# A tuned decoder trunk on one core: kept sums for a second set of seven products, and a norm row made three units later

## The chip, the cores and the metric

The kernel runs on one core of one Trainium2 chip. The metric is the device time of one execution in microseconds, from the first to the last instruction of the core with what lies around it. TensorE (PE) multiplies matrices, VectorE (DVE) and ScalarE (ACT) work on tiles elementwise, GpSimd (POOL) and SyncE (SP) mostly issue transfers here.

## The reference

Two layers over 256 tokens of width 2048. Layer 0 mixes with chunked gated linear attention, layer 1 with forgetting attention, whose keys, values and forget gates come from a projection of the normed stream between the layers. Each layer ends with a gated MLP, 5632 wide, with a causal convolution of width 3 between the up projection and the gate. All is float32.

```python
def fox_shared_kv(x, g_kv, w_kv, b_f):
    hs = rmsnorm(x, g_kv)
    k, v, fl = split_cols(hs @ w_kv, [FOX_WIDTH, FOX_WIDTH, FOX_HEADS])
    ...

def conv_ffn(h, w_up, conv_w, conv_b, w_down):
    u = causal_dwconv(h @ w_up, conv_w, conv_b)
    a, val = split_cols(u, [FFN_HIDDEN, FFN_HIDDEN])
    return (jax.nn.silu(a) * val) @ w_down

def reference(x, ...):
    for i in range(DEPTH):
        if i == N_A_LAYERS:
            fk, fv, fc = fox_shared_kv(x, fox_kv_norm, fox_w_kv, fox_b_f)
        ...
        h = rmsnorm(x, norm_ffn[i])
        x = x + conv_ffn(h, ffn_w_up[i], ffn_conv_w[i], ffn_conv_b[i], ffn_w_down[i])
    return rmsnorm(x, norm_final)
```

## The kernel before

**Products in three.** Every float32 operand is held as a rounded high part and the rest, its low part, and a product is three matmuls: high by high, low by high, high by low. Activations are split once. Weights arrive from memory in units of 512 KB (128 x 1024) and are split as they come: ACT casts the raw unit to `whi` (L229, or L377 in a set of seven), DVE subtracts to get `wlo` (L230, L378). PE reads both as the moving operand, 512 columns a matmul.

**An up pair.** The up projection is made in 11 pairs a layer, j = 0, 4, ..., 40, each by `pair_steps`. A pair has 16 input chunks of 128, so 16 units, and fills four results of 128 tokens x 512 columns; a plain unit is 12 matmuls. They lie in accumulator banks named p1 to p7 and x. The banks take turns from pair to pair, so that in some pairs p1 is printed as `acc` and in others as `ps_o`.

**A set of seven products.** At chunk 6 (SEVEN_UP) two units go together: 2 x 2 blocks of tokens and columns over two input chunks are multiplied with seven block products instead of eight, 21 matmuls instead of 24. It needs sums of the inputs (`usum`, made once a layer by `input_sums` and `token_sums`) and of the weights: the units land in `ra` and `rb` (`raw2`, two buffers in turn), the first halves are cast as w1 (512 columns) and w2, then four DVE subtractions (L427 to L430) turn `ra` and `rb` into block differences, which are cast as w3 and w4. So a set has four casts at L377 instead of two at L229. Its products p1, p5, p6, p7 have banks of their own. After a pair's last set `early` runs: two ACT copies of bank p1 (L1472 plain, L1473 scaled), four DVE adds that combine p6, p7 and p5 (L1474 to L1477), three ACT scales (L1479). At the pair's end `late` adds the results (L1483), and DVE transposes them (L1435).

**A second set.** The first pair after each part's down pairs (j = 20 and j = 32) has one more set, at chunk 11 (`more`, SEVEN_MORE). For it the sums of chunks 11 and 12 are made anew each time, in the buffer of a down projection's sums (`dsum0`): twice a layer.

**Work beside.** What follows the up projection (24 convolution taps on ACT at L1384, adds at L1391, silu L1397, product L1404, the splits L516 and L517, sums L672 and L673) is handed out in small steps by `tick(share)` while PE works on the next pairs. `drive` gives a share of 1.45 a unit.

**What sets the order.** The program is put in order by a scheduler that simulates the engines before anything runs. Work inside `tc.high_priority(offset=AHEAD)` is placed earlier, `tc.issue_after` sets a floor. Each engine then executes its list in that order. The order of ACT's list around a set is therefore an outcome of that simulation, and a small edit can reorder it.

**The norm row.** The projection for the shared keys (`two_tm([fk(0), fk(1)], ...)`, then `fk(2)`) needs the norm of the stream only when its results are read. `nx.row` (L589 to L598) spreads the norm over partitions: DVE builds a diagonal `dg` twice, PE multiplies it with ones into `ps_t`, ACT copies `row` out. Before it is hooked behind unit 2 of `fk(1)`.

## Time and profile before

| | before |
|---|---|
| three runs, us | 2221.61, 2224.04, 2224.32 (median 2224.04) |
| the profiled execution, us | 2221.88, its span 2220.1 |
| PE busy, us | 2207.2 (99%) in 10323 instructions |
| DVE busy, us | 1788.5 (81%) |
| ACT busy, us | 1418.8 (64%) |
| POOL busy, us | 136.1 (6%) |
| granted TensorE clock, mean | 0.999 |

The span runs from the first to the last instruction, so it is 1.8 us shorter than the execution's own time. In a row of the profile `L402 PE MATMUL acc<-whi,B` reads: line 402, engine, operation, the tile written and the tiles read, without buffer numbers. `whi` and `wlo` are weights, `B`, `A`, `mix` and `more` split activations, `usum` and `dsum` sums of them. A busy time is a sum over instructions; matmuls overlap, so a group's mean of 389 ns is not the time from one start to the next.

### The profile page before, as it was taken

What the parts mean: (1) busy time and instruction counts of PE and PEld (TensorE: products, weight loads), DVE (VectorE), ACT (ScalarE), POOL (GpSimd) and SP (SyncE); (2) the same over time, 40 slices, a digit from 0 to 9 for tenths busy, and PEclk for the clock granted to TensorE, in tenths of its full rate; (3) what the DMA queues carried; (4) which work ended last, traced back from release to release, by engine and by line L of the source; (5) the groups of instructions that cost most, each with busy time, mean ns of one, the idle gap of its engine ahead of it and who ended that gap; (6) DMA issues with size and microseconds to landing.
All of it is one profiled execution on the core that took longest, in us unless ns stands there. A gap on an engine that the chain in (4) does not pass through costs nothing.

```text
span 2220.1 us, 30058 instructions
## 1 busy us (share of the span) xinstructions
PE 2207.2 (99%) x10323; PEld 1853.8 (84%) x10323; DVE 1788.5 (81%) x2654; ACT 1418.8 (64%) x2257; POOL 136.1 (6%) x257
## 2 busy tenths in 40 slices
PE   9999999999999999999999999999999999999998
PEld 7888888888888888888887998888888888888886
DVE  7768977688897888888978569668888888888896
ACT  6655664556787468656865455555787647665874
POOL 0000000001100000001110000000101000100100
PEclk9999999999999999999999999999999999999999
DMA  9767667778777567667777767777677757766674
GB/s 356 245 223 222 192 191 242 248 231 253 229 243 258 185 221 244 227 225 240 226 250 244 233 203 244 224 240 244 218 240 246 240 196 239 234 236 222 225 258 150
DMA packets 165633, 515.47 MB, mean 232 GB/s; under 512 B 20700, under 2 KB 41832, under 8 KB 165480
## 3 DMA queue, kind: packets, MB, share of 16 engines
q1 hardware_dynamic: 148488, 461.36, 63.6%
q0 software_dynamic: 16416, 51.40, 7.6%
q8 instruction: 81, 1.33, 0.2%
q10 hardware_dynamic: 576, 0.79, 0.1%
q14 instruction: 72, 0.59, 0.1%
HBM read 469.68 MB, written 43.79 MB: 231 GB/s over the span
## 4 chain that ended last, share of the span: by engine, by line
PE 95%; issue 2%; DVE 1%; DMA 1%; ACT 0%; POOL 0%; DVEq 0%; ACTq 0%; POOLq 0%
PE acc L402 30%; PE acc L333 23%; PE ps_s L402 15%; PE ps_o L402 7%; PE ps_t L402 7%; PE acc L305 3%; PE acc L260 3%; PE acc L363 2%; PE acc L258 1%; PE ps_s L333 1%; DVE wlo L230 0%; PE ps_s L1011 0%; DMA raw<-wp 0%; DMA fvt<-far 0%; PE ps_o L686 0%
## 5 line engine op out<-in xcount | busy, mean ns | idle before, releaser
L230 DVE TENSOR_TENSOR wlo<-raw,whi 128x1024 fp32r<-128x1024 f32 (+4 forms) x739 | 876.8, 1196 | 256.6 <-ACT whi L229 232.6
L229 ACT ACTIVATE whi<-raw 128x1024 fp32r<-128x1024 f32 (+4 forms) x739 | 760.4, 1037 | 447.4 <-PE acc L333 166.3
L333 PE MATMUL acc<-whi,B 128*128 128x512 f32 (+3 forms) x1248 | 292.0, 370 | 0.0
L377 ACT ACTIVATE whi<-raw 128x1024 fp32r<-128x1024 f32 (+1 forms) x136 | 129.8, 954 | 190.7 <-PE acc L402 75.5
L333 PEld LDWEIGHTS acc<-whi,B 128*128 128x128 f32 x1248 | 227.1, 188 | 28.0
L378 DVE TENSOR_TENSOR wlo<-raw,whi 128x1024 fp32r<-128x1024 f32 (+1 forms) x136 | 148.0, 1091 | 63.3 <-ACT whi L377 58.8
L402 PE MATMUL acc<-whi,mix 128*128 128x512 f32 x764 | 194.6, 389 | 0.0
L402 PE MATMUL acc<-whi,B 128*128 128x512 f32 x750 | 193.0, 389 | 0.0
L402 PEld LDWEIGHTS acc<-whi,mix 128*128 128x128 f32 x764 | 143.3, 188 | 30.2 <-ACT whi L229 0.2
L402 PEld LDWEIGHTS acc<-whi,B 128*128 128x128 f32 x750 | 140.8, 188 | 29.6
L333 PE MATMUL acc<-wlo,B 128*128 128x512 f32 (+3 forms) x624 | 158.6, 369 | 0.0
L333 PEld LDWEIGHTS acc<-wlo,B 128*128 128x128 f32 x624 | 114.6, 188 | 14.5
L1384 ACT ACTIVATE tap<-yzu,cw 128x256 f32<-128x256 f32 x264 | 123.5, 531 | 1.5 <-DMA yzu<-far 1.5
L1384 ACT ACTIVATE tap<-fvt,cw 128x256 f32<-128x256 f32 x264 | 123.3, 529 | 0.8 <-DMA fvt<-far 0.8
L1391 DVE TENSOR_TENSOR tap<-tap,tap 128x1024 f32<-128x1024 f32 x88 | 107.3, 1219 | 1.1 <-ACT tap L1384 1.0
L402 PE MATMUL acc<-wlo,mix 128*128 128x512 f32 x382 | 107.5, 389 | 0.0
L402 PE MATMUL acc<-wlo,B 128*128 128x512 f32 x375 | 107.3, 389 | 0.0
L402 PE MATMUL ps_s<-whi,mix 128*128 128x512 f32 x386 | 106.1, 389 | 0.0
L402 PE MATMUL ps_s<-whi,B 128*128 128x512 f32 x342 | 93.5, 389 | 0.0
L402 PEld LDWEIGHTS ps_s<-whi,mix 128*128 128x128 f32 x386 | 72.5, 188 | 15.3
L402 PEld LDWEIGHTS acc<-wlo,mix 128*128 128x128 f32 x382 | 71.7, 188 | 15.0
L402 PEld LDWEIGHTS acc<-wlo,B 128*128 128x128 f32 x375 | 70.4, 188 | 14.7
(498 smaller groups left out, 3802.3 us busy)
## 6 DMA issues: line engine op xcount, KB each, us to landing
raw<-wp SPq DMA_DIRECT2D x743, 512.0 KB, 4.5
fvt<-far POOLq DMA_DIRECT2D x100, 128.0 KB, 5.3
raw<-wp SPq DMA_DIRECT2D x32, 384.0 KB, 3.5
far<-yu POOLq DMA_DIRECT2D x22, 512.0 KB, 5.8
far<-yzu POOLq DMA_DIRECT2D x22, 512.0 KB, 5.4
yzu<-far POOLq DMA_DIRECT2D x88, 128.0 KB, 5.0
raw<-wp SPq DMA_DIRECT2D x24, 388.0 KB, 4.7
x<-xtok SPq DMA_DIRECT2D x8, 512.0 KB, 6.6
```

Of the source, the lines that this page charges most:

```text
L229: casts.append(S.activation(hi[:, s], raw[:, s], AF.Copy))
L230: lows.append(V.tensor_tensor(lo[:, s], raw[:, s], hi[:, s].bitcast(F32), ALU.subtract))
L258: mm = TE.matmul(acc[p][c][:, :T], w[:, s], both[:, 0, :], start=False, stop=end and j == 3)
L260: mm = TE.matmul(acc[p][c], w[:, s], both, start=u == j == 0, stop=end and j == 3)
L305: mm = TE.matmul(acc[b][:, :n], src[kcs[j] - base][:, part, b * P : (b + 1) * P], w, start=u == 0 and low == part == j == 0, stop=u == end ...
L333: mm = TE.matmul(acc[b][:, :n], src[kc - base][:, part, b * P : (b + 1) * P], ready[low][:, j * n : (j + 1) * n], start=i == low == part = ...
L363: mm = TE.matmul(acc[b][:, :n], src[kc - base][:, part, b * P : (b + 1) * P], w, start=i == low == part == j == 0, stop=i == end and low = ...
L377: casts.append(S.activation(hi[:, :n], src, AF.Copy))
L378: lows.append(V.tensor_tensor(lo[:, :n], src, hi[:, :n].bitcast(F32), ALU.subtract))
L402: r = TE.matmul(bank[name], x, w, start=name not in begun, stop=last)
L1384: S.activation(by_run(taps[i][:, s, c, i:]), zs[slot][:, :, 2 * c + s], AF.Copy if i else AF.Identity, bias=0.0 if i else w[3], scale=w[2 ...
L1391: V.tensor_tensor(taps[0], taps[0], taps[n][:, :, :, :T], ALU.add)
```

## The change

1. `MORE_IN = (1, 5, 6, 8, 9)`: the pairs j = 4, 20, 24, 32 and 36 have a set at chunk 11 beside the one at chunk 6. Before, only 20 and 32 had. So j = 4, 24 and 36 are new, in both layers.
2. The sums of chunks 11 and 12 are made once a layer, at unit 13 of pair 0, into a tile of their own (`usum11`) that stays for the layer. The two makings a layer into `dsum0` go.
3. Pairs in `MORE_IN` hand out the work beside with a share of 1.7 instead of 1.45.
4. For room, the mask's part that only the linear attention uses is a tile `gmask` of that stage's pool, loaded on POOL's queue instead of SP's.
5. `nx.row` runs after unit 3 of `fk(2)`, instead of after unit 2 of `fk(1)`.

```diff
--- before.py
+++ after.py
@@ -35,6 +35,7 @@
 SEVEN_UP = (6,)
 SEVEN_DOWN = {4: 0, 10: 1, 20: 0, 34: 1}
 SEVEN_MORE = 11
+MORE_IN = (1, 5, 6, 8, 9)
 
 
 LEVELS = (64, 16, 4)
@@ -157,11 +158,10 @@
 
     gains = const.tile([P, G_N], F32, name="gains")
     part = const.tile([P, C_N], F32, name="part")
-    mask = const.tile([P, M_N], F32, name="mask")
+    mask = const.tile([P, M_SCAN], F32, name="mask")
     ident = mask[:, M_ID : M_ID + P]
     ones = mask[:, M_ONE : M_ONE + P]
     foxmask = mask[:, M_FOX : M_FOX + T]
-    scanmask = mask[:, M_SCAN : M_SCAN + T]
 
     def gain(name, i):
         c = C_GAIN[name] + i
@@ -808,7 +808,7 @@
                     for i in range(KC):
                         nc.sync.dma_start(xf[i], xt[i])
                     nc.sync.dma_start(part, par)
-                    nc.sync.dma_start(mask[:, M_FOX:], msk[:, M_FOX:])
+                    nc.sync.dma_start(mask[:, M_FOX:], msk[:, M_FOX:M_SCAN])
         with tc.issue_after(nrm.made.ins):
             for i in range(KC):
                 split(bufB, i, xf[i], gain("mix0", i))
@@ -833,6 +833,8 @@
         h, mix = bufB, bufA
         with tc.tile_pool(name="gla", bufs=1) as gp:
             scratch[0] = gp
+            gmask = gp.tile([P, M_N - M_SCAN], F32, name="gmask")
+            nc.gpsimd.dma_start(gmask, msk[:, M_SCAN:])
 
             ks = [place("A", 8 + i, "ks", F32) for i in range(2)]
             gq1, gk1 = place("A", 10, "gq1", F32), place("A", 11, "gk1", F32)
@@ -882,7 +884,7 @@
                     mz = gp.tile([P, T], F32, name="gm", tag="tmp", bufs=5)
                     V.tensor_scalar(mz, ps[:, :T], bias, 0.0, ALU.add, ALU.min)
                     V.tensor_tensor(mz, mz, e, ALU.subtract)
-                    V.tensor_tensor_scan(bc[:, c, :], scanmask, mz, 0.0, ALU.mult, ALU.add)
+                    V.tensor_tensor_scan(bc[:, c, :], gmask[:, :T], mz, 0.0, ALU.mult, ALU.add)
                 return bc
 
 
@@ -1030,12 +1032,13 @@
                 for b in range(2):
                     S.activation(a3[:64, b, 64:], ps[64 * b : 64 * (b + 1), P : P + 64], AF.Copy)
                 ins = inside[hd % 2]
-                eye = mask[:, M_EYE:].bitcast(I32).unsqueeze(1).to_broadcast(ins.shape)
+                eye = gmask[:, M_EYE - M_SCAN :].bitcast(I32).unsqueeze(1).to_broadcast(ins.shape)
                 V.copy_predicated(ins, eye, ps[:, 192:320].rearrange("p (b t) -> p b t", b=2))
                 for li, B in enumerate(LEVELS):
                     H = B // 4
                     p3 = levels[li].rearrange("p (b c) -> p b c", b=2)
-                    m3 = mask[:, M_LVL + NVER * li : M_LVL + NVER * (li + 1)].bitcast(I32)
+                    at0 = M_LVL - M_SCAN + NVER * li
+                    m3 = gmask[:, at0 : at0 + NVER].bitcast(I32)
                     o4 = ins.rearrange("p b (n t) -> p b n t", t=B)
                     for i, (o, w) in enumerate(VERSIONS):
                         og = o4[:, :, :, (i + 1) * H :]
@@ -1162,11 +1165,12 @@
             def query_input(i):
                 split_turned(hq, i, (*stash, spare[1])[i // 4], "mix1")
 
-            two_tm([fk(0), fk(1)], 8, 2, {(1, 2): nx.row,
-                                          (1, 3): lambda: nx.land(spare[1]), (1, 5): nx.take})
+            two_tm([fk(0), fk(1)], 8, 2, {(1, 3): lambda: nx.land(spare[1]), (1, 5): nx.take})
             step = fk(2)
             for u in range(8):
                 step(u)
+                if u == 3:
+                    nx.row()
                 query_input((u + 12) % KC)
             cs = fp.tile([P, T], F32, name="fc")
             cc = fp.tile([P, 2, FOX_H], F32, name="fcc")
@@ -1411,12 +1415,12 @@
 
             product = [None]
 
-            def input_sums(k, tag="usum", at=None):
+            def input_sums(k):
 
                 r = fp.tile([P, 2, T], F32, name="cv", tag="cv")
                 for s in range(2):
                     V.tensor_tensor(r[:, s, :], h[k + s][:, 0, :].bitcast(F32), h[k + s][:, 1, :].bitcast(F32), ALU.add)
-                t = held(tag, k if at is None else at)
+                t = held("usum", k)
                 token_sums(r, t)
                 return t
 
@@ -1461,7 +1465,10 @@
                     credit[0] -= cost
                     step()
 
-            def up_pair(j, more={}):
+            def sets_of(j):
+                return (*SEVEN_UP, SEVEN_MORE) if j // 4 in MORE_IN else SEVEN_UP
+
+            def up_pair(j):
 
                 count[2] += 1
                 turns = [turn(j + 2 * h_, 8) for h_ in range(2)]
@@ -1483,26 +1490,29 @@
                         V.scalar_tensor_tensor(u[b, h_], a, scale(b), u[b, h_], ALU.mult, ALU.add)
                     turns[h_](b, u[b, h_])
 
-                return pair_steps(where["up", l, j], h, {**up_sums, **more}, count[2] % 2, pool, early, late)
+                return pair_steps(where["up", l, j], h, {k: up_sums[k] for k in sets_of(j)}, count[2] % 2, pool, early, late)
 
             def first(k):
                 {2: lambda: nx.land(landing[0]), 3: nx.take, 8: nx.col,
                  9: lambda: nx.land(landing[1]), 11: nx.take}.get(k, int)()
+                if k == 13:
+                    up_sums[SEVEN_MORE] = input_sums(SEVEN_MORE)
                 tick(0)
 
             def drive(steps, share=1.45):
                 for k in steps:
                     tick(share if k >= 0 else 0.0)
+
+            def drive_up(j):
+                drive(up_pair(j), 1.7 if j // 4 in MORE_IN else 1.45)
 
             up_sums = {k: input_sums(k) for k in SEVEN_UP}
             for k in up_pair(0):
                 first(k)
             done = 4
-            more = {}
             for p, (lo, hi) in enumerate(PARTS[:-1]):
                 while done < hi + 4:
-                    drive(up_pair(done, more))
-                    more = {}
+                    drive_up(done)
                     done += 4
                 src = [m[c % RING] for c in range(lo, hi)]
                 for f in (0, 2):
@@ -1510,11 +1520,9 @@
                     drive(down_pair(l, p, f, src, {c - lo: t for c, t in sums.items() if f}, count[2] % 2, pool,
                                     lambda: (temps(0), temps(1))))
                 sums.clear()
-                more = {SEVEN_MORE: input_sums(SEVEN_MORE, "dsum", 0)}
             lo, hi = PARTS[-1]
             while done < hi:
-                drive(up_pair(done, more))
-                more = {}
+                drive_up(done)
                 done += 4
             p = len(PARTS) - 1
             src = [m[c % RING] for c in range(lo, hi)]
```

The lines move by 7 from the FFN on: L1384 becomes L1388, L1397 becomes L1401, L1472 and L1473 become L1479 and L1480, L1479 becomes L1486. In the listings below a name's buffer number may differ between the kernels (`raw_5469` before is `raw_5488` now).

**ACT's list, the set at chunk 6 of the third up pair (j = 8) of layer 0.** The pair before it, j = 4, has one set before and two now. The rows at L377 are the casts of w1 (512 columns), w2, w3 and w4, in this order; L1472/L1473 (now L1479/L1480) are the copies of the pair's own bank p1. Before:

```order
L377 ACTIVATE whi<-raw_5469 128x512
L377 ACTIVATE whi<-raw_5470 128x1024
L1397 ACTIVATE tap_4575<-tap_4575 128x2x256
L516 ACTIVATE mix_3451<-cv 128x256
L516 ACTIVATE mix_3458<-cv 128x256
L377 ACTIVATE whi<-raw_5469 128x1024
L377 ACTIVATE whi<-raw_5470 128x1024
L229 ACTIVATE whi<-raw 128x1024
L1384 ACTIVATE tap_4576<-fvt,cw 128x4x2x32
L1384 ACTIVATE tap_4577<-fvt,cw 128x4x2x32
L1384 ACTIVATE tap_4576<-fvt,cw 128x4x2x32
L1472 ACTIVATE fvt<-ps_o 128x512
```

Now:

```order
L377 ACTIVATE whi<-raw_5488 128x512
L377 ACTIVATE whi<-raw_5489 128x1024
L1401 ACTIVATE tap_4577<-tap_4577 128x2x256
L1479 ACTIVATE fvt<-ps_o 128x512
L1480 ACTIVATE fvt<-ps_o,ny 128x512
L377 ACTIVATE whi<-raw_5488 128x1024
L516 ACTIVATE mix_3453<-cv 128x256
L516 ACTIVATE mix_3460<-cv 128x256
L377 ACTIVATE whi<-raw_5489 128x1024
L229 ACTIVATE whi<-raw 128x1024 x2
```

Both copies of p1, which stood behind w4 and a further cast, now stand ahead of w3; the splits at L516 stand between w3 and w4. The sets of j = 8 and j = 40 have this order in both layers.

**The same place of the other following pair, j = 28 of layer 0** (j = 28 of layer 1 reads the same). Now:

```order
L377 ACTIVATE whi<-raw_8040 128x512
L377 ACTIVATE whi<-raw_8041 128x1024
L1479 ACTIVATE fvt<-acc 128x512
L1480 ACTIVATE fvt<-acc,ny 128x512
L1401 ACTIVATE tap_4577<-tap_4577 128x2x256
L377 ACTIVATE whi<-raw_8040 128x1024
L672 ACTIVATE dsum<-cv 128x512
L377 ACTIVATE whi<-raw_8041 128x1024
```

Here the silu stands between the copies and w3, and a sum of the down projection (L672) between w3 and w4.

**The second set of a new two-set pair (j = 4 of layer 0).** Now:

```order
L377 ACTIVATE whi<-raw_5217 128x512
L377 ACTIVATE whi<-raw_5218 128x1024
L377 ACTIVATE whi<-raw_5217 128x1024
L1479 ACTIVATE fvt<-acc 128x512
L1480 ACTIVATE fvt<-acc,ny 128x512
L377 ACTIVATE whi<-raw_5218 128x1024
```

The copies stand behind w3 and ahead of w4 here. That is also the order in six sets of the kernel before, j = 12 and j = 28 of layer 0 among them.

**PE's list at the set of j = 8, layer 0.** `B_105` and `B_106` are chunks 6 and 7. The rows `ps_o<-whi,B_105` and `ps_o<-wlo,B_105` are product p1 (w1), `B_106` and the first `usum` rows into `acc` are w2, `ps_s<-whi,usum` is w3, `ps_t<-whi,usum` and the following `acc<-whi,B_106` are w4. Before:

```order
L402 MATMUL acc<-whi,B_104 128x512 x8
L402 MATMUL acc<-wlo,B_104 128x512 x4
L402 MATMUL ps_o<-whi,B_105 128x512 x2
L402 MATMUL ps_o<-wlo,B_105 128x512
L402 MATMUL acc<-whi,B_106 128x512 x2
L402 MATMUL acc<-wlo,B_106 128x512
L402 MATMUL acc<-whi,usum 128x512 x2
L402 MATMUL acc<-wlo,usum 128x512
L402 MATMUL ps_s<-whi,usum 128x512 x4
L402 MATMUL ps_t<-whi,usum 128x512 x2
L402 MATMUL acc<-whi,B_106 128x512 x2
L402 MATMUL ps_s<-wlo,usum 128x512 x2
```

Now:

```order
L402 MATMUL ps_o<-whi,B_105 128x512 x2
L402 MATMUL acc<-wlo,B_103 128x512 x4
L402 MATMUL acc<-whi,B_104 128x512 x8
L402 MATMUL acc<-wlo,B_104 128x512 x4
L402 MATMUL acc<-whi,B_106 128x512 x2
L402 MATMUL acc<-whi,usum 128x512 x2
L402 MATMUL ps_o<-wlo,B_105 128x512
L402 MATMUL acc<-wlo,B_106 128x512
L402 MATMUL acc<-wlo,usum 128x512
L402 MATMUL ps_s<-whi,usum 128x512 x4
L402 MATMUL ps_t<-whi,usum 128x512 x2
L402 MATMUL acc<-whi,B_106 128x512 x2
```

The last matmul of p1, `ps_o<-wlo,B_105`, has moved behind the first rows of w2: from it to the first matmul of w3 it is now 3 matmuls (7 before), and to the first of w4 7 (11 before).

**PE's list at the norm row.** Before, in `fk(1)`:

```order
L333 MATMUL acc<-whi,B_111 128x512 x2
L333 MATMUL acc<-whi,B_112 128x512 x2
L333 MATMUL acc<-whi,B_111 128x512 x2
L596 MATMUL ps_t<-dg,onesr 128x256
L333 MATMUL acc<-whi,B_112 128x512
L596 MATMUL ps_t<-dg,onesr 128x256
L333 MATMUL acc<-whi,B_112 128x512
```

Now, in `fk(2)`, some 90 matmuls later:

```order
L333 MATMUL acc<-wlo,B_106 128x512
L333 MATMUL acc<-wlo,B_105 128x512
L333 MATMUL acc<-wlo,B_106 128x512
L596 MATMUL ps_t<-dg,onesr 128x256 x2
L333 MATMUL acc<-whi,B_107 128x512 x2
L333 MATMUL acc<-whi,B_108 128x512 x2
```

The two L596 matmuls left the middle of a unit and stand between two units.

## The prediction

> **What bounds the kernel now.** I read the page's first part, then the chain of waits, then the windows of single up pairs, then the timeline around one set.
>
> ```profile
> span 2220.1 us, 30058 instructions
> PE 2207.2 (99%) x10323; PEld 1853.8 (84%) x10323; DVE 1788.5 (81%) x2654; ACT 1418.8 (64%) x2257; POOL 136.1 (6%) x257
> ...
> PE 95%; issue 2%; DVE 1%; DMA 1%; ACT 0%; POOL 0%; DVEq 0%; ACTq 0%; POOLq 0%
> ```
>
> PE is busy in 2207.2 of 2220.1 us, and 95% of the chain is PE. So a matmul that goes is a gain, and a wait that PE did not have is a loss, nearly one for one. There is little else: all idle time of PE together is 12.9 us.
>
> ```profile
> 758.30:800.80 42.50, 42.50 (x188) 34.96 (x188) 33.80 (x38) 22.95 (x26) 0.00 (x0) 1.00 0.57 191
> 800.80:843.80 43.00, 43.00 (x191) 35.51 (x190) 35.22 (x44) 32.66 (x52) 5.50 (x10) 1.00 0.79 248
> 843.80:886.80 43.00, 43.00 (x191) 35.53 (x190) 37.31 (x45) 32.79 (x53) 5.47 (x10) 1.00 0.74 236
> 935.10:977.50 42.40, 42.40 (x188) 34.99 (x187) 39.05 (x50) 20.74 (x24) 0.00 (x0) 1.00 0.69 228
> 1020.50:1063.40 42.90, 42.90 (x190) 35.43 (x189) 38.05 (x49) 32.87 (x53) 5.46 (x10) 1.00 0.77 246
> ```
>
> The columns are the window, its length, then busy time and count of PE, PEld, DVE, ACT and POOL, and the clock. These are up pairs of layer 0, from one pair's first matmul to the next pair's: j = 20 and j = 32 (42.5 and 42.4 us, two sets), j = 24, 28 and 40 (43.0, 43.0 and 42.9, one set). PE fills every one of them. What the reader must also see is ACT: 22.95 and 20.74 us in the two-set pairs, some 33 in the others. The same windows for the convolution taps alone (L1384 on ACT):
>
> ```profile
> 758.30:800.80 42.50, 0.00 (x0) 1.00 0.57 191
> 800.80:843.80 43.00, 11.21 (x24) 1.00 0.79 248
> 935.10:977.50 42.40, 0.00 (x0) 1.00 0.69 228
> ```
>
> The pairs with two sets carried no taps; the new ones do. So DVE and ACT have not yet been seen under both loads at once.
>
> **The gain of a second set.** It replaces 24 matmuls by 21, of which 12 read the sums.
>
> ```profile
> 857.78 1.07 PE L402 MATMUL ps_s<-whi,B 128*128 128x512 f32 x4
> 858.69 0.61 PE L402 MATMUL ps_t<-whi,B 128*128 128x512 f32 x2
> 862.11 1.10 PE L402 MATMUL acc<-whi,usum 128*128 128x512 f32 x4
> 863.05 0.63 PE L402 MATMUL acc<-wlo,usum 128*128 128x512 f32 x2
> ```
>
> Four plain matmuls take 858.69 - 857.78 = 0.91 us, 0.227 each; four on sums 863.05 - 862.11 = 0.94, 0.235 each. A set therefore gains 3 x 0.227 - 12 x 0.008 = 0.58 us, which is what the windows differ by (0.5 to 0.6). Six new sets: **-3.5 us**. Bounds: 0.5 and 0.6 each, -3.0 to -3.6.
>
> **The gain of the norm row.**
>
> ```profile
> PE ps_t L596 <- DVE dg L594: 2.0, 1, 2.0
> ```
> ```profile
> 1199.94 1.52 PE L333 MATMUL acc<-whi,B 128*128 128x512 f32 x6
> 1203.46 0.38 PE L596 MATMUL ps_t<-dg,onesr 128*128 128x256 f32 x1 [2.00 <-DVE dg L594]
> 1204.27 1.09 PE L333 MATMUL acc<-wlo,B 128*128 128x512 f32 x4
> ```
> ```profile
> 1200.36 1.23 DVE L230 TENSOR_TENSOR wlo<-raw,whi 128x1024 fp32r<-128x1024 f32 x1
> 1201.57 1.23 DVE L230 TENSOR_TENSOR wlo<-raw,whi 128x1024 fp32r<-128x1024 f32 x1
> ```
>
> Six matmuls from 1199.94 at 0.227 end their turn at 1201.30; the next starts at 1203.46. The gap is 2.16 us, and it waits for DVE's diagonal. Moved behind unit 3 of fk(2), some 90 matmuls or 20 us later, the row finds it ready: DVE's own order is unchanged there. What would be late next are the weights: the `wlo` read at 1204.27 was done at 1201.59, so 2.68 us ahead; 2.16 earlier it is still 0.5 ahead, and the next, done at 1202.80, is read eight matmuls later, at 1202.11 + 1.82 = 1203.9. I take the whole **-2.2 us**; if that slack is eaten, the bound is -1.1.
>
> **The cost: two waits in the pair after each new one.** This is the term that decides. In j = 8, 28 and 40 of both layers ACT's list now has the two copies of p1 ahead of the cast w3, and PE's list has w3 three matmuls behind p1's last. ACT cannot start the copies before PE ends p1, and PE cannot start w3 before ACT has cast it. The pair j = 28 of before shows how long this takes, with the copies one cast later:
>
> ```profile
> 857.46 0.72 ACT L516 ACTIVATE mix<-cv 128x256 fp32r<-128x256 f32 x2 [1.97 <-DVE cv L1404]
> 858.15 1.07 ACT L377 ACTIVATE whi<-raw 128x1024 fp32r<-128x1024 f32 x1
> ...
> 860.50 0.39 PE L402 MATMUL acc<-wlo,B 128*128 128x512 f32 x1
> ...
> 860.93 0.60 ACT L1472 ACTIVATE fvt<-acc 128x512 f32<-128x512 f32 x1 [1.72 <-PE acc L402]
> 861.42 0.68 ACT L1473 ACTIVATE fvt<-acc,ny 128x512 f32<-128x512 f32 x1
> 862.00 1.06 ACT L377 ACTIVATE whi<-raw 128x1024 fp32r<-128x1024 f32 x1
> 862.94 1.06 ACT L229 ACTIVATE whi<-raw 128x1024 fp32r<-128x1024 f32 x1
> 863.09 1.23 DVE L378 TENSOR_TENSOR wlo<-raw,whi 128x1024 fp32r<-128x1024 f32 x1 [2.04 <-ACT whi L377]
> 863.51 0.63 PE L402 MATMUL acc<-whi,usum 128*128 128x512 f32 x2
> ```
>
> Count from the start of p1's last matmul (860.50). The first copy starts at +0.43, the second at +0.92, the cast behind them at +1.50, and it ends at +2.56; the subtraction that waits for it starts 0.03 later, and I give PE 0.04. Here the cast was w4, which PE wanted 13 matmuls after p1's last, at 863.51: 0.45 us to spare. So in the second sets of the new pairs, where the copies stand in this same place and w4 is again 13 matmuls away, I cost the wait at nothing; if its 0.45 us are gone, the loss there is what goes beyond them.
>
> In j = 8 and j = 40 it is w3 that is ready at +2.60, and PE wants it 3 matmuls after, at 2 x 0.227 + 0.235 = +0.69: PE stands **1.91 us**. Then two splits (857.46 to 858.15, 0.69) stand ahead of w4's cast: it starts at 1.50 + 0.94 + 0.69 = +3.13 and is ready at 3.13 + 1.06 + 0.04 = +4.23. PE, which began w3 at +2.60, wants w4 four matmuls later, at +3.54: another **0.69**. Together 2.60 us, in four pairs 10.4.
>
> In the two pairs j = 28 the silu stands ahead of w3 and a sum ahead of w4.
>
> ```profile
> L1397 ACT ACTIVATE tap<-tap 128x512 f32<-128x512 f32 x44 | 27.2, 617 | 0.8 <-DVE tap L1391 0.8
> L672 ACT ACTIVATE dsum<-cv 128x512 fp32r<-128x512 f32 x12 | 7.5, 624 | 1.7 <-PE ps_t L402 1.1 <-DVE cv L467 0.6
> ```
>
> Both have means near 0.62, and follow-on starts 0.11 earlier (0.60 against 0.49 at the copy), so 0.51 each. w3 is ready at +3.11, a stall of 2.42; w4 at 2.01 + 0.94 + 0.51 + 1.10 = +4.56 against 4.05, 0.51 more. Together 2.93, twice 5.9. Sum of the stalls: **+16.3 us**. Lower bound, if everything behind w3 is hidden: 4 x 1.91 + 2 x 2.42 = 12.5. Upper bound with DVE late as well: the rival below. Behind the waiting cast ACT's list holds the casts of the next units, and DVE's their `wlo`; PE stands for longer than these are delayed, so I count them nothing.
>
> **Edits that I cost at nothing.** The kept sums drop 2 x 7 DVE operations, under DVE's cover of 81%; the mask's load moves to POOL, which is 6% busy; the share 1.7 hands steps out earlier and shows in the order already.
>
> **DVE.** A new set adds four 512-wide subtractions and replaces two lows by four.
>
> ```profile
> L427 DVE TENSOR_TENSOR raw<-raw 128x512 f32<-128x512 f32 x34 | 23.5, 690 | 0.6
> L378 DVE TENSOR_TENSOR wlo<-raw,whi 128x1024 fp32r<-128x1024 f32 x102 | 124.9, 1225 | 51.2 <-ACT whi L377 49.5
> L378 DVE TENSOR_TENSOR wlo<-raw,whi 128x512 fp32r<-128x512 f32 x34 | 23.4, 689 | 12.2 <-ACT whi L377 9.3 <-PE ps_t L402 2.7
> ```
>
> That is 4 x 0.69 + 0.69 + 3 x 1.23 - 2 x 1.23 = 4.7 us. On 37.3 to 38.05 of a one-set pair it gives 42.0 to 42.8, against 42.4 of PE: DVE has no room left in the new pairs. That it queues up work for the next pair is part of why the copies stand where they stand, and on the chip it may add to the stall; I take nothing, since the copies' chain alone is longer.
>
> **The sum.** -3.5 - 2.2 + 16.3 = +10.6 us on the profiled execution's 2221.88 us gives 2232.5; on the median 2224.04, which lies 2.16 above it, 2234.6. The runs of before lie half at the one and half at the other, so I forecast **2233.5 us**, with its own range 2229 to 2239.
>
> **The rivals.**
> 1. *The waits are hidden, and only the gains are left.* PE is ahead of nothing else in those pairs, so without a stall -3.5 - 2.2 = -5.7: 2223.0, the middle of the runs, becomes 2217.3, faster. It decides at +0.69 us behind p1's last matmul: w3 would have to be cast by then. For it speaks that no wait of PE above some tenths stands in any up pair of before. Against it: the row at 860.93 starts at +0.43 and its second copy ends at +1.60, before the cast even begins. It needs that I have read the wrong tile or place in the lists. 11%.
> 2. *Only w3 waits.* If w4's cast is in time, +12.5 - 5.7 = +6.8: 2229.8. Against it stand the two splits between the casts. 10%.
> 3. *DVE becomes the bound.* By the counts of its list and the durations above, DVE has 31 to 31.7 us of work from a new second set to the next set, for 129 matmuls or 29.3 us of PE. If the lag of up to 2.4 us reaches the subtractions L428 to L430 ahead of w3 and w4, some 1.5 us more in each of six pairs: 9 more, 2242.5. Against it: in j = 28 above, w3's cast ended at 859.22 and was wanted at 862.11, a lead of 2.9 us that covers the lag. 10%.
> 4. *The stalls cost less than half.* If PE finds the lists' order only in some of the six, say two of them, about +5.4 - 5.7: no change, 2223. 5%.
> 5. *The clock falls after each stall.*
>
> ```profile
> 1.46 4.21 PE L186 MATMUL ps_o<-B 128*128 128x512 f32 x9 [1.46 <-DVE B L183]
> 5.46 1.91 PE L305 MATMUL acc<-whi,A 128*128 128x512 f32 x4
> ```
>
> The first nine matmuls start 0.444 us apart, 0.217 more than later. If each of six stalls brought nine such matmuls, 6 x 9 x 0.217 = 11.7 more: 2245. Against it: after the gap before 1203.46 the matmuls from 1204.27 come four in 0.93 us, full pace. 2%. The Trainium skill, page "TensorE: Matmul & The Clock Gate", section "What's actually happening", has the array fall to half rate after an idle window of about 3.4 us and stay there for about as long. By that rule the stalls here, 1.9 and 0.7 us with matmuls between, stay below the window, and the sum would be as it is; the trace agrees with it for a gap of 2.16 us and shows no longer one.
>
> **How the numbers follow.** The forecast has 62%. A measurement of this kernel can tell 0.2%, 4.4 us, from no change. Slower by more: the forecast and rivals 2, 3 and 5, 84%, less 2% for the part of them that ends within 4.4 us, 82%. Faster: rival 1, 11%. Within: rival 4 and those 2%, 7%. The range leaves out rivals 1 and 5 and reaches from 2224 (rival 4) to 2243 (rival 3).
>
> **What would show it.** In the changed kernel's trace the pairs j = 8, 28 and 40 take 45.5 to 46 us instead of 43.0; in each stand two waits of PE for ACT `whi` L377 at L402, near 1.9 (2.4) and 0.6 us, and ACT's first copy (L1479) waits for PE directly ahead of w3's cast. The new pairs themselves take 42.4. The wait at L596 is gone. I would be wrong in the main if PE shows no gap at w3, wrong in size if the wait for w3 is for DVE L428 (rival 3), and wrong in the gains if new pairs take more than 42.6 us.

## The result and the profile after

| | before | changed |
|---|---|---|
| median, us | 2224.04 (2221.3 to 2224.5, 5 runs) | 2242.97 (2241.7 to 2245.7, 5 runs) |
| ratio | 1 | 1.0091, 95% interval 1.0076 to 1.0106 |
| the profiled execution, us | 2221.88, span 2220.1 | 2245.66, span 2243.7 |
| mean granted clock | 0.999 | 0.995 |
| PE instructions | 10323 | 10305 |

The change makes the kernel 18.9 us slower; the forecast was 9.5. The profiled execution is the slowest of the five, 23.6 us of span above the one of before, so the account below is of that larger difference.

The page of the changed kernel, its first part and its chain of waits:

```profile
span 2243.7 us, 30090 instructions
PE 2215.5 (99%) x10305; PEld 1854.0 (83%) x10305; DVE 1811.9 (81%) x2676; ACT 1427.9 (64%) x2267; POOL 136.7 (6%) x258
...
PE 92%; issue 2%; DMA 2%; DVE 1%; ACT 1%; POOL 0%; SPq 0%; DVEq 0%; ACTq 0%; POOLq 0%
```

PE's busy time went up by 8.3 us although it has 18 matmuls fewer: some of them took longer. Its idle time went from 12.9 to 28.2 us. The windows of the pair j = 8 before, then of the new pair j = 4 and of the pair j = 8 behind it now (PE, PEld, DVE, ACT, POOL, then the clock):

```profile
543.50:586.50 43.00, 43.00 (x190) 35.48 (x190) 37.31 (x47) 33.13 (x54) 5.47 (x10) 1.00 0.77 246
```
```profile
500.60:543.10 42.50, 42.50 (x188) 34.98 (x188) 33.91 (x38) 27.96 (x41) 5.45 (x10) 1.00 0.72 217
543.10:588.80 45.70, 43.60 (x191) 35.41 (x190) 43.43 (x57) 38.05 (x65) 5.46 (x10) 1.00 0.77 255
```

The new pair takes 42.4 us from its first matmul to the next pair's, as it should; so do the other five. The pair behind it takes 45.6 instead of 43.0, and 47.0 to 47.6 in the other five places. DVE has 43.43 us to do there instead of 37.31, and only 33.91 in the new pair itself. The timeline around its set, PE, ACT and DVE:

```profile
559.32 0.63 ACT L1401 ACTIVATE tap<-tap 128x512 f32<-128x512 f32 x1 [4.87 <-DVE tap L1395]
559.87 0.69 DVE L428 TENSOR_TENSOR raw<-raw,raw 128x512 f32<-128x512 f32 x1
560.53 0.39 PE L402 MATMUL ps_o<-wlo,B 128*128 128x512 f32 x1
560.96 0.60 ACT L1479 ACTIVATE fvt<-ps_o 128x512 f32<-128x512 f32 x1 [1.00 <-PE ps_o L402]
561.45 0.68 ACT L1480 ACTIVATE fvt<-ps_o,ny 128x512 f32<-128x512 f32 x1
562.02 1.06 ACT L377 ACTIVATE whi<-raw 128x1024 fp32r<-128x1024 f32 x1
562.97 0.72 ACT L516 ACTIVATE mix<-cv 128x256 fp32r<-128x256 f32 x2
563.13 1.20 PE L402 MATMUL ps_s<-whi,usum 128*128 128x512 f32 x4 [1.74 <-ACT whi L377]
563.58 1.05 ACT L377 ACTIVATE whi<-raw 128x1024 fp32r<-128x1024 f32 x1
564.69 0.73 PE L402 MATMUL ps_t<-whi,usum 128*128 128x512 f32 x2 [0.35 <-ACT whi L377]
```

This is the forecast's chain step by step. Counted from p1's last matmul at 560.53, the copies start at +0.43 and +0.92, the cast of w3 at +1.49, and PE has w3 at +2.60. What the raw block needed was ready at 560.56, when L428 ended; the cast started 1.46 us later, behind the copies. In the pair j = 28 the same happens, and then something more:

```profile
863.32 0.40 PE L402 MATMUL ps_s<-wlo,usum 128*128 128x512 f32 x1
865.97 2.93 PE L402 MATMUL acc<-whi,usum 128*128 128x512 f32 x6 [2.26 <-ACT whi L377]
868.70 0.86 PE L402 MATMUL ps_s<-whi,B 128*128 128x512 f32 x2
869.40 0.63 PE L402 MATMUL acc<-wlo,usum 128*128 128x512 f32 x2
```

Six matmuls from 865.97 take 868.70 - 865.97 = 2.73 us, 0.455 each, where six at pace take 1.4. The windows say why, in the clock column (behind PE's busy time and count):

```profile
860.00:863.40 3.40, 3.40 (x17) 1.00 0.90 241
863.40:866.00 2.60, 0.34 (x3) 0.96 0.50 202
866.00:870.00 4.00, 4.00 (x11) 0.60 0.42 117
1618.60:1624.00 5.40, 5.04 (x14) 0.68 0.45 118
```

After the stand the granted clock is 0.60 over 4 us: the clock halves, and matmuls start 0.427 us apart. It did so behind five of the six stands (a stand is a time in which PE starts nothing), not behind that of j = 8 in layer 0.

**Where the 23.6 us come from**, worked out from the starts of all matmuls in the two traces (the time beyond 0.227 us wherever two starts are more than 0.24 apart):

| term | us | forecast |
|---|---|---|
| waits for w3, six pairs (2.14, 2.66, 2.14, 2.14, 2.66, 2.14 from start to start) | +12.5 | +12.5 |
| waits for w4, five pairs (0.43 to 0.53) | +2.6 | +3.8 |
| matmuls at half clock behind five of them, and first matmuls after each wait | +8.8 | 0 |
| gaps at other places of the FFN (1129, 1531, 2188 us) | +2.6 | 0 |
| gaps in the shared keys (1176 to 1193 us) | +2.8 | 0 |
| the norm row's wait gone | -2.2 | -2.2 |
| six sets | -3.5 | -3.5 |

### The profile page after: what moved, and what is told of

It is laid out like the page before. It is cut to its first block, busy times and chain, and to the rows that moved or that the text cites. A ratio compares the mean times of both kernels' runs of the same rounds, so it can differ in the third digit from the quotient of the medians.

```text
span 2243.7 us, 30090 instructions
## 1 busy us (share of the span) xinstructions
PE 2215.5 (99%) x10305; PEld 1854.0 (83%) x10305; DVE 1811.9 (81%) x2676; ACT 1427.9 (64%) x2267; POOL 136.7 (6%) x258
## 4 chain that ended last, share of the span: by engine, by line
PE 92%; issue 2%; DMA 2%; DVE 1%; ACT 1%; POOL 0%; SPq 0%; DVEq 0%; ACTq 0%; POOLq 0%
PE acc L402 29%; PE acc L333 23%; PE ps_s L402 14%; PE ps_o L402 7%; PE ps_t L402 7%; PE acc L305 3%; PE acc L260 3%; PE acc L363 2%; PE ps_s L333 2%; PE acc L258 1%; ACT whi L377 1%; DMA far<-blk 1%; DVE wlo L378 0%; DMA fvt<-far 0%; DMA far<-tblk 0%
## 5 line engine op out<-in xcount | busy, mean ns | idle before, releaser
L230 DVE TENSOR_TENSOR wlo<-raw,whi 128x1024 fp32r<-128x1024 f32 (+4 forms) x727 | 861.9, 1193 | 268.0 <-ACT whi L229 244.3
L229 ACT ACTIVATE whi<-raw 128x1024 fp32r<-128x1024 f32 (+4 forms) x727 | 747.7, 1037 | 446.0 <-PE acc L333 157.1
L377 ACT ACTIVATE whi<-raw 128x1024 fp32r<-128x1024 f32 (+1 forms) x160 | 151.1, 951 | 190.1 <-PE acc L402 68.5
L378 DVE TENSOR_TENSOR wlo<-raw,whi 128x1024 fp32r<-128x1024 f32 (+1 forms) x160 | 173.9, 1089 | 84.3 <-ACT whi L377 76.3
L1388 ACT ACTIVATE tap<-fvt,cw 128x256 f32<-128x256 f32 x264 | 122.9, 529 | 1.8 <-DMA fvt<-far 0.9
L1388 ACT ACTIVATE tap<-yzu,cw 128x256 f32<-128x256 f32 x264 | 123.2, 530 | 0.8 <-DVE tap L1395 0.8
L402 PEld LDWEIGHTS acc<-wlo,B 128*128 128x128 f32 x371 | 69.6, 188 | 14.6
```

The costliest lines, as they stand in the source:

```text
L229: casts.append(S.activation(hi[:, s], raw[:, s], AF.Copy))
L230: lows.append(V.tensor_tensor(lo[:, s], raw[:, s], hi[:, s].bitcast(F32), ALU.subtract))
L377: casts.append(S.activation(hi[:, :n], src, AF.Copy))
L378: lows.append(V.tensor_tensor(lo[:, :n], src, hi[:, :n].bitcast(F32), ALU.subtract))
L402: r = TE.matmul(bank[name], x, w, start=name not in begun, stop=last)
L1388: S.activation(by_run(taps[i][:, s, c, i:]), zs[slot][:, :, 2 * c + s], AF.Copy if i else AF.Identity, bias=0.0 if i else w[3], scale=w[2 ...
```

## The experiments

Times are medians; the kernel before was run beside each group (2223.1 to 2223.3).

**1. The copies held behind w4.** In the up pair's `early`:

```diff
-                    S.activation(u[0, 1], bank["p1"], AF.Copy)
-                    S.activation(u[0, 0], bank["p1"], AF.Copy, scale=scale(0))
+                    with tc.issue_after(casts[-1].ins):
+                        S.activation(u[0, 1], bank["p1"], AF.Copy)
+                        S.activation(u[0, 0], bank["p1"], AF.Copy, scale=scale(0))
```

> The changed kernel with one edit: in `early` of the up pairs the two ACT copies of bank p1 get a floor behind the cast of w4. The lists of ACT then have both copies behind w4 in every up pair, all six new sets stay. Theory A (the order of ACT's list makes PE stand, and the TensorE clock halves for some matmuls after the stand): the six clusters of gaps in the pairs j = 8, 28 and 40, which took 2.66, 3.99, 4.26, 4.26, 4.49 and 4.22 us in the profile of the changed kernel (23.9 us in all), are gone with their half-rate matmuls; the time falls by 20 to 24 us from 2243.0 to 2219 to 2223. Rival B (DVE has no room for a second set beside the taps, and the copies only stood where the wait was anyway): PE waits at the same places for DVE L428 or L430 or for wlo L378 instead, at least half of the 23.9 us stays, 2231 or more.

Measured: 2236.51 (2232.5 to 2239.1), ratio 1.0053 (1.0039 to 1.0066). The six clusters (a cluster is all gaps around one set, summed beyond the pace) are 1.64, 3.69, 1.63, 1.81, 6.22 and 1.72 us, 16.7 instead of 23.9. Only 6.5 us of the time went, as rival B had it, so the order is not the whole cause. The timeline of the same set, and ACT's waits around it:

```profile
560.08 0.69 DVE L428 TENSOR_TENSOR raw<-raw,raw 128x512 f32<-128x512 f32 x1
560.20 0.73 ACT L516 ACTIVATE mix<-cv 128x256 fp32r<-128x256 f32 x2 [2.24 <-DVE cv L1408]
560.88 1.06 ACT L377 ACTIVATE whi<-raw 128x1024 fp32r<-128x1024 f32 x1
561.74 0.69 DVE L430 TENSOR_TENSOR raw<-raw 128x512 f32<-128x512 f32 x1
562.00 1.19 PE L402 MATMUL ps_s<-whi,usum 128*128 128x512 f32 x4 [0.61 <-ACT whi L377]
562.55 1.06 ACT L377 ACTIVATE whi<-raw 128x1024 fp32r<-128x1024 f32 x1 [0.60 <-DVE raw L430]
```
```profile
ACT tap L1401 <- DVE tap L1395: 3.3, 1, 3.3
ACT mix L516 <- DVE cv L1408: 2.2, 1, 2.2
ACT whi L377 <- DVE raw L430: 0.6, 1, 0.6
```

Now ACT waits for DVE three times in a row: for the tap sum, for the gate's product, for the difference L430. L428 ends at 560.77; PE would have wanted w3 cast at about 561.2. DVE is late, and the trace shows no wait of its own over the ten us before.

**2 and 3. The parts without new pairs.** First everything but the new pairs (`MORE_IN = (5, 8)`), then the norm row's move alone in the kernel before.

> The changed kernel with MORE_IN = (5, 8): the kept sums, the mask's part as a tile of its own, the share 1.7 and the later norm row are all there, but only the pairs j = 20 and 32 have a second set, as before. Theory A: no gap in the up pairs, the wait at L596 (2.16 us) gone, so 2224.0 - 2.2 = 2221.9, at most 1 us more if the kept sums' work at pair 0 of layer 1 costs the 1.2 us that stood there in the changed kernel. Rival B (the row's new place or the kept sums bring the new gaps at the down projection and the shared keys, 1128 to 1193 us of the changed kernel, some 3 us): 2224 to 2225, with those gaps in the profile.

> The kernel before with the norm row behind unit 3 of fk(2) and nothing else. Theory A: the gap of 2.39 us before L596 is gone and nothing takes its place: 2224.0 - 2.2 = 2221.9. Rival B: the wait moves to a later reader (wlo L230 or the row itself), less than 1 us gained, 2223 or more.

Measured: 2221.31 (ratio 0.9991, 0.9983 to 1.0) and 2220.79 (0.9990, 0.9981 to 0.9999). The row's move gains 2.3 us on the median, near the 2.2 that its wait had cost; the interval leaves 0.2 to 4.2 open, and in the profile, where the wait is gone, 1.1 us of other gaps in the shared keys came in. The kept sums neither gain nor lose what can be told. The whole loss comes with the three new pairs of each layer. Neither has a gap in an up pair.

**4. The order alone, on the kernel before.** A hook makes the two copies ahead of w3 in j = 8, 28 and 40:

```diff
-                w3 = split_more(ra, 1024)
+                gate = mid(bank) if mid is not None and done else None
+                with tc.issue_after(gate.ins) if gate is not None else nullcontext():
+                    w3 = split_more(ra, 1024)
```

> The kernel before, without a new set; only in the pairs j = 8, 28 and 40 of both layers the two copies of p1 are made before the cast w3, which gets a floor behind them. PE's list has w3 seven matmuls behind p1's last here (three in the changed kernel). Theory A (the order alone is enough): w3 is ready 2.60 us after the start of p1's last matmul and wanted at 1.61, so each of the six pairs has a gap of about 1.0 us beyond the pace, PE waiting for ACT whi L377; 2224 + 6 = 2230, and the clock stays whole after gaps this short. Rival B (it takes the second set's work on DVE): no gap above 0.3 us, 2224 to 2225.

Measured: 2230.66, ratio 1.0032 (1.0020 to 1.0044). Six gaps of 1.23 us from start to start, all six the same, each with PE waiting for ACT `whi` L377, and none followed by a half-rate matmul: 6 x 1.11 = 6.7 us in the up pairs. The order costs its wait with no second set in sight. One stretch in the middle of this profile is at half rate all the same: the norm row's wait, 2.39 us from start to start before, is 2.83 here, and five matmuls 0.427 apart follow it.

**5. DVE relieved.** Experiment 1 with one addition fewer:

```diff
-steps += [(1.0, lambda: add_tap(1)), (1.0, lambda: add_tap(2)), (0.5, silu),
+steps += [(1.0, lambda: add_tap(2)), (0.5, silu),
```

> The first kernel of the experiments (copies of p1 held behind w4, all six new sets) without one of the two tap additions (`add_tap(1)`) in every pair: the convolution's second tap is left out of the result. That takes two DVE additions of 1.14 us, 2.3 us, out of every up pair and changes nothing on PE. Theory C (DVE is short of time between the second set of a new pair and the next set; L428 and L430 come late there whatever the order on ACT): the six clusters of 1.6 to 6.2 us (16.7 in all) fall to under 0.5 us each; 2236.5 - 15 = 2221, 2218 to 2224. Rival D (something else holds the weights back, ACT's list or the buffers): at least half of the 16.7 us stays, 2229 or more.

Measured: 2221.93, ratio 0.9996 (0.9987 to 1.0006). Of the 16.7 us two clusters of 0.97 and 0.99 (j = 28) and one of 0.56 stay, more than expected there, and 0.7 and 0.4 stand in two other places. The windows of the same two pairs:

```profile
500.00:543.00 43.00, 43.00 (x190) 35.41 (x189) 34.83 (x41) 29.36 (x44) 5.45 (x10) 1.00 0.70 222
543.00:586.00 43.00, 43.00 (x191) 35.52 (x190) 37.75 (x45) 35.90 (x61) 5.46 (x10) 1.00 0.80 258
```

PE is full again in both, at DVE's 37.75 of 43 us against 43.43 of 45.7 in the changed kernel. DVE's time is the second cause.

**6 and 12. The additions on GpSimd**, one of two, then both (`nc.gpsimd.tensor_tensor`), with the copies held. Nothing is left out.

> The first kernel of the experiments with the addition `add_tap(1)` of every pair on GpSimd instead of DVE; nothing is left out. Theory C: DVE gets 2.3 us a pair, as without the addition, and if GpSimd needs less than some 5 us for one and does not slow DVE, 2221 to 2225 (the two would be a version at or below the kernel before). Rival D: the addition comes late on GpSimd, the gate's steps behind it move into the next set, or DVE's instructions take longer while GpSimd works; 2230 or more, and the mean of DVE L230 above 1.25 us.

> The first kernel of the experiments (copies held, six new sets) with both tap additions of every pair on GpSimd; nothing left out. With one there, 10.2 us of gaps stayed in the up and down pairs, behind DVE L428 and L430. Theory C: DVE gets 4.6 us a pair back, less what its instructions lengthen while GpSimd works (L230 1.22 to 1.26 us with one, so perhaps 1.30), and the gaps fall below 3 us: 2219 to 2223, at or below the kernel before. Rival D: two additions of 2.28 us in a row delay the gate's steps past the next set, or DVE slows by more than it is spared; 2228 or more.

Measured: 2230.13 (ratio 1.0033, 1.0019 to 1.0047) and 2256.19 (1.0146, 1.0129 to 1.0163). The groups of lines, first of the one, then of the other:

```profile
L1395 POOL TENSOR_TENSOR tap<-tap,tap 128x1024 f32<-128x1024 f32 x44 | 100.3, 2279 | 588.6 <-ACT tap L1388 563.0 <-DVE cv L466 25.7
L230 DVE TENSOR_TENSOR wlo<-raw,whi 128x1024 fp32r<-128x1024 f32 x661 | 825.9, 1260 | 234.5 <-ACT whi L229 219.7 <-PE acc L258 2.7 <-issue 2.5
```
```profile
L1395 POOL TENSOR_TENSOR tap<-tap,tap 128x1024 f32<-128x1024 f32 x88 | 222.6, 2529 | 442.4 <-ACT tap L1388 420.1 <-DVE yzu L1439 9.7 <-DVE temp L1491 9.5
L230 DVE TENSOR_TENSOR wlo<-raw,whi 128x1024 fp32r<-128x1024 f32 x661 | 886.9, 1354 | 227.2 <-ACT whi L229 212.5 <-PE acc L258 2.7 <-PE ps_s L402 2.2
```

An addition takes 2.28 us there against 1.21 on DVE, and DVE's subtraction L230 lengthens from 1.22 to 1.26 and 1.35 us on the mean over the whole kernel. With one, the time falls by 6.4 us against experiment 1, though the addition itself takes longer there, which speaks for DVE's time as the cause and not the length of the chain behind the additions. The kernel before is not reached, as rival D had it. With both it loses, and the second expectation was wrong by 33 us. The Trainium skill, page "GPSIMD Engine Reference", section "1. Specifications", says that GpSimd shares its SBUF interfaces with VectorE and contends with DVE instructions that have two SBUF inputs; L230 has two, and the trace agrees.

**7. The share back at 1.45**, copies held.

> The first kernel of the experiments with the share back at 1.45 in the two-set pairs. Theory C: what DVE has to do up to the next set is only handed out later, within the same stretch; the six clusters stay within a third of their 16.7 us, 2231 to 2241. Rival E (the share of 1.7 alone overfills DVE in the new pairs): the clusters mostly go, 2224 or less.

Measured: 2241.29, ratio 1.0085 (1.0069 to 1.0101). That is at the upper end of what theory C gave. The six clusters take 18.4 us, and a seventh of 1.16 stands in pair 0 of layer 1. ACT's waits at j = 8 of layer 0 name DVE alone:

```profile
ACT whi L377 <- DVE raw L428: 6.0, 1, 6.0
ACT whi L377 <- DVE raw L430: 0.4, 1, 0.4
```

The larger share is not what overfills DVE; with the smaller one the kernel is 4.8 us slower than experiment 1, and DVE's subtractions are what ACT waits for.

**8. A ruler for the clock**, on the kernel before: the hook of experiment 4 with n further copies.

> A ruler for the clock, on the kernel before: in eight one-set pairs of each layer w3's cast stands behind the copies of p1 and behind n more copies of the same bank (n = 0 to 7 in another order in each layer), so that PE stands about 1.0 + 0.49 n us beyond its pace in one place a pair, with full work around it. Theory A (a stand of some 2 us can halve the clock, and where it does depends on more than its length): no half-rate matmuls (0.427 us from start to start) behind n = 0 and 1, behind some of n = 2 to 4, behind all of n = 5 to 7; each time 6 to 9 of them, 1.2 to 1.8 us. Time 2224 + 44 (gaps) + 10 to 18 = 2278 to 2286. Rival F (only a stand of about 3.4 us counts): half-rate matmuls behind n = 5 to 7 alone. Rival G (the stand is not the cause, only the new kernel's own work is): none at all, 2268.

Measured: 2295.48, ratio 1.0339 (1.0321 to 1.0358), above all three; a copy lengthened the stand by 0.63 us, not 0.49. The gaps from start to start, and how many matmuls behind them started 0.427 apart (full half-rate steps, counted in the trace):

| n | 0 | 1 | 2 | 3 | 4 | 5 | 6 | 7 |
|---|---|---|---|---|---|---|---|---|
| layer 0, gap us | 1.23 | 1.85 | 2.86 | 3.11 | 3.74 | 4.37 | 5.00 | 6.14 |
| half-rate | 0 | 0 | 7 | 0 | 7 | 5 | 7 | 8 |
| layer 1, gap us | 1.23 | 1.86 | 2.49 | 3.12 | 4.11 | 4.37 | 5.00 | 5.63 |
| half-rate | 0 | 0 | 7 | 0 | 7 | 11 | 5 | 11 |

Two rows of its timeline show that length alone does not decide, a stand of 3.12 us and one of 2.49, each with what follows:

```profile
830.82 0.40 PE L402 MATMUL acc<-wlo,usum 128*128 128x512 f32 x1
833.94 1.20 PE L402 MATMUL ps_s<-whi,usum 128*128 128x512 f32 x4 [2.72 <-ACT whi L377]
834.97 0.41 PE L402 MATMUL ps_t<-whi,usum 128*128 128x512 f32 x1
...
1969.31 0.40 PE L402 MATMUL ps_s<-wlo,usum 128*128 128x512 f32 x1
1971.80 1.99 PE L402 MATMUL acc<-whi,usum 128*128 128x512 f32 x6 [2.09 <-ACT whi L377]
1973.59 1.06 PE L402 MATMUL ps_s<-whi,mix 128*128 128x512 f32 x2
1974.44 1.06 PE L402 MATMUL acc<-wlo,usum 128*128 128x512 f32 x2
```

Behind the first, four matmuls take 1.03 us; behind the second, pairs take 0.85. The traces' records of the clock, which the clock column averages, tell them apart. In all fourteen profiles of this case they change only at multiples of 3.41 us from the first change on, and a half-rate stretch in the middle of a run is one or two such steps long. The steps around the two stands:

```profile
829.52:832.93 3.41, 1.70 (x8) 1.06 (x6) 0.00 (x0) 2.96 (x6) 0.00 (x0) 1.00 0.02 6
832.93:836.34 3.41, 2.40 (x10) 1.91 (x11) 2.42 (x3) 3.41 (x5) 0.00 (x0) 1.00 0.00 0
1969.57:1972.98 3.41, 1.32 (x6) 0.91 (x6) 1.20 (x2) 3.37 (x5) 2.18 (x4) 1.00 0.28 78
1972.98:1976.39 3.41, 3.41 (x10) 2.66 (x9) 3.41 (x4) 3.41 (x7) 0.00 (x0) 0.50 0.28 87
```

The stand of 3.11 us is shared by two steps, in which six and ten matmuls start (15 at full pace); that of 2.49 lies in one almost whole, five start there, and the next step is at half clock. Counted over every step of the fourteen traces from the first clock change to the last matmul: all 27 steps with five starts or fewer were followed by half clock, four of the eight with six, and none with seven or more.

**9. The order without DVE's shortage.** The changed kernel, copies not held, one addition fewer as in experiment 5.

> The changed kernel itself (copies of p1 not held) without `add_tap(1)`, so that DVE has its 2.3 us a pair back; the convolution's second tap is left out of the result. The order now has the copies ahead of w3 in j = 8 and j = 40 of both layers (w3 four matmuls behind p1's last) and ahead of w4 only in j = 28 (nine behind). Theory A with C (two causes, each enough: the order on ACT costs its wait even where DVE has time): 2.60 - 0.92 = 1.7 us at w3 and up to 0.7 at w4 in four pairs, 0.5 in two, 8 to 11 us, with half-rate matmuls behind some; 2222 + 8 to 14 = 2230 to 2236. Rival C alone (the order costs nothing once DVE is in time): 2220 to 2224.

Measured: 2227.08, ratio 1.0016 (1.0007 to 1.0025): faster than A expected and slower than C alone, 5.2 us above experiment 5. The waits at w3 of j = 8 and 40 are 1.92 us from start to start in all four, 1.69 beyond the pace, as worked out; 0.48 beyond the pace in j = 28. There is no second wait at w4 and no half-rate matmul behind any, and these are what A had added on top. So each cause is enough for a wait. The order here is not quite that of the changed kernel: with an addition fewer the scheduler put the copies behind w3 in j = 28.

**10. Sets further apart.** One set at chunk 11 instead of 6 in j = 8, 12, 16 and 28, without the new set of j = 36.

> The changed kernel with the sets further apart and nothing left out: MORE_IN = (1, 5, 6, 8), so j = 36 has one set again, and the pairs behind j = 4 and j = 24 up to the next down pairs (j = 8, 12, 16 and 28) have their one set at chunk 11 instead of 6, from the sums that are kept anyway. DVE then has 16 units instead of 11 between the second set of a new pair and the next set. Theory C: no clusters in the up pairs; four new sets at 0.58 and the norm row's 2.3 give 2223.1 - 2.3 - 2.3 = 2218.5, 2217 to 2221. Rival: the set at chunk 11 runs into the pair's end or into the next pair's first units, clusters of over 1 us appear there, 2225 or more.

Measured: 2248.59, ratio 1.0115 (1.0098 to 1.0131): worse than the change. The rival's time is met, but not by its reason. The timeline at the set of j = 8 shows the one there, which neither side had:

```profile
566.17 0.63 ACT L378 ACTIVATE whi<-raw 128x512 fp32r<-128x512 f32 x1 [0.18 <-DMA raw<-wp]
567.33 5.26 ACT L1389 ACTIVATE tap<-fvt,cw 128x256 f32<-128x256 f32 x12
572.50 1.99 ACT L378 ACTIVATE whi<-raw 128x1024 fp32r<-128x1024 f32 x2
575.85 0.69 DVE L430 TENSOR_TENSOR raw<-raw,raw 128x512 f32<-128x512 f32 x1
577.35 1.06 ACT L378 ACTIVATE whi<-raw 128x1024 fp32r<-128x1024 f32 x1 [1.81 <-DVE raw L431]
578.46 0.73 PE L403 MATMUL ps_t<-whi,usum 128*128 128x512 f32 x2 [1.75 <-ACT whi L378]
```

(Lines are one higher here.) At chunk 11 the set meets the taps: twelve of them stand between the cast of w1 and that of w2, DVE's list waits for w2, and L430 and L431 come after it. DVE had room: it waits 3.73 us for w2's cast. ACT's order took it.

**11. The changed kernel once more.**

> The changed kernel unaltered, profiled a second time. Theory A (the same list of work gives the same stands of PE; whether the clock then halves depends on where in time they fall): the six gaps at w3 come out within 0.05 us of the first profile (2.14, 2.66, 2.14, 2.14, 2.66, 2.14), but the set of places with half-rate matmuls differs (five of six in the first profile, not behind the first). Rival F (length alone decides): the same five of six.

Measured: 2241.25, one run. The gaps at w3 are 2.14, 2.66, 2.14, 2.14, 2.66 and 2.14 us again. Half-rate matmuls follow only three of them (j = 28 and 40 of layer 0, j = 28 of layer 1), not five. The gaps are a property of the lists; the halving depends on where they fall among the clock's steps, and these begin elsewhere in each run (in the two profiles the first change is at 5.63 and at 6.00 us, while the first stand begins at 560.99 and 561.11).

The lowest median of all is that of experiment 3, the norm row alone: 2220.79 against 2223.12 of the kernel before beside it.

## Why the prediction was right and wrong

**Right: the direction, and the waits at w3.** The forecast that w3 is ready 2.60 us after p1's last matmul, 1.91 late (2.42 in j = 28), was met to 0.01 us in all six pairs, and experiments 4 and 9 show the order to be enough for a wait there. The gain of the sets came as forecast: the new pairs take 42.4 us instead of 43.0. The row's wait is gone, and experiment 3 agrees with its gain. The time of the pair behind, 45.5 to 46 us in the forecast, came in the first profile only in j = 8 of layer 0 (45.6), the one place where the clock stayed whole.

**A size off: w4.** The term gave 0.69 and 0.51 us; 0.43 to 0.53 came in five pairs and none in one. In j = 8 the two splits took 0.61 us instead of 0.69, and PE's first matmul after the wait 0.34 instead of 0.23. In j = 28 of layer 0 the half clock made w3's own matmuls last until w4 was there.

**Wrong: "The clock falls after each stall" was a rival at 2% and a cost of nothing in the sum.** It fell behind five of six stands in one profile and three in another, and with the first matmuls after the waits it is 8.8 of the 23.6 us, some 8 of it the half clock alone. This is the largest term of the table that the sum left out. The step that failed took one gap, that before 1203.46, for the rule. A gap of 2.39 us that leaves the clock whole says only that it can: nine matmuls started in the step of 3.41 us that held most of it. The same wait of 2.83 us in experiment 4, with four starts in its step, halved the clock. Experiment 8 shows gaps of 2.49 and 2.86 that halve it and of 3.11 and 3.12 that do not. The rival's price, nine matmuls for each of six, 11.7, was not far off for one run. The Trainium skill's page "TensorE: Matmul & The Clock Gate" had been drawn on there for an idle window of about 3.4 us. The same section, "What's actually happening", also has that window run freely. This bears more, and the traces agree: the clock's steps of 3.41 us lie elsewhere in each run. But the step need not be idle. By the count of experiment 8, five starts in one, a third of the full fifteen, were always few enough. So every stand of 3.74 us or more was followed by half rate, none of 1.92 or less by itself, and between them its place decided; in the first experiment two stands of 1.2 and 1.13 us in one step, with six starts, were enough too. That j = 8 of layer 0 escaped in both profiles was luck of this kind: seven and eight matmuls started in its step.

**Wrong in place, and in what it would mean: DVE.** The forecast gave DVE 42.0 to 42.8 of the 42.4 us of a new pair and took nothing for it, "since the copies' chain alone is longer". In all six new pairs DVE had only 33.0 to 34.1 us; the work came in the pair behind, 43.4 to 45.1 us against 37.2 to 38.2 before. A reason stands in the kernel, though no run tests it: `early` runs behind a pair's last set, and a set at chunk 11 moves it five units back. At w3 of j = 8 the forecast's reason held: L428 was ready 1.46 us before the cast began. But removing the order alone kept 16.7 of 23.9 us. Four medians show both causes: 2242.97 with both, 2236.51 without the order (experiment 1), 2227.08 without the addition (9), 2221.93 without either (5). The order is worth 6.5 or 5.2 us, the addition 15.9 or 14.6. The two nearly add up, and DVE's is the larger; but experiment 9 has another order at j = 28 too, so its 15.9 are not DVE's time alone.

**Missed: 5.4 us elsewhere.** The gaps at 1129, 1531 and 2188 us and in the shared keys were not looked for. The one at 1531 is again a w4 behind DVE L430, in pair 0 of layer 1. Those at 1129 wait for ACT's split L516. The gaps in the shared keys are not the new pairs' doing: they take 0.9 us before, 3.4 in experiment 2, without any new pair, 0.1 in experiment 5, and 3.7 and 3.0 in two profiles of the changed kernel. Why they vary was not settled.

The median's 18.9 against the profile's 23.6 us is in the clock for a part: the second profile, with two places of half rate fewer, has 22.8 us of gaps in the FFN instead of 26.6, of which some 3 are the clock's.

## What to carry to other kernels

Before saving matmuls at the price of other engines' work, sum that work over the stretch up to the next tight place, not over the kernel: DVE was busy 81% overall, and had 43 to 45 us to do in a pair that PE can finish in 43. Read the lists that a scheduler made, at every place where an engine reads what another has just written; a copy that moves ahead of a cast costs a round trip, and that can be worked out to 0.01 us. Where TensorE is the bound, price a stand of more than 2 us, or shorter ones close together, with a chance of half clock behind it, some 1.6 us more each time.

## What the runs showed of the hardware

- The TensorE clock changed only at steps of 3.41 us, whose place differs from run to run. It was half in the step after each of 27 with five matmul starts or fewer (15 at full pace), after four of eight with six, after none with more. So the same stand of 2.14 us halved it in one profile and not in the next. The half rate (0.427 us from start to start) lasted 5 to 11 matmuls.
- The same two-input float32 subtraction of 128 x 1024 took DVE 1.22, 1.26 and 1.35 us on the mean as GpSimd did none, 44 and 88 additions of 2.28 and 2.53 us.
- A second profile of one kernel repeated its six gaps at w3 to 0.002 us.
